# Quarter sums, feature stores and one weight sum of a SwiGLU block are issued at other places

## The chip, the cores and the metric

One NeuronCore of a Trainium2 chip runs the whole block. The metric is the device time of the program in microseconds (us), from its start to its end; lower is better. The engines are named as the profile names them: PE (TensorE, matrix products), PEld (its weight loads), DVE (VectorE), ACT (ScalarE), POOL (GpSimd) and SP (SyncE, which only issues DMAs here). ACTq, SPq and POOLq are the queues of an engine's instructions before they run; a DMA that an engine issues stands in its queue among its other instructions.

## What is computed

One layer of a streaming encoder over 1024 tokens of width 1024, in float32: a normed input projection, eight heads of causal attention with forget gates beside a pooling mixer, an output projection with residual, then a SwiGLU feed-forward with residual and a last norm. The change lies in the feed-forward, of which this is the reference:

```python
def rmsnorm(x, g):
    xf = x.astype(jnp.float32)
    y = xf * lax.rsqrt(jnp.mean(xf * xf, axis=-1, keepdims=True) + EPS)
    return (y * g.astype(jnp.float32)).astype(x.dtype)
...
        h2 = rmsnorm(x, norm2_g[layer])
        gate = jnp.einsum('bsd,df->bsf', h2, w_gate[layer])
        up = jnp.einsum('bsd,df->bsf', h2, w_up[layer])
        x = x + jnp.einsum('bsf,fd->bsd', jax.nn.silu(gate) * up, w_down[layer])
    return rmsnorm(x, final_g)
```

The inner width D_FF is 2816, that is 22 blocks of 128, or 11 pairs of blocks.

## The kernel before

**Precision.** Every float32 product is made of three products of a reduced type. `split` (L119 to L121) writes a high part on ACT (a copy into that type) and a low part on another engine, DVE as a rule (source minus high part). `mm3` (L157 on) then adds high by high (L161), high by low (L162) and low by high (L163) in one PSUM bank. In the profile nearly all matmuls carry these three lines, and all high and low parts L120 and L121. A "page" is the high and the low part of one weight operand.

**Seven products for eight.** Gate and up weights and the normed tokens are cut in two by two blocks, and each such product is made of seven block products instead of eight, P1, P2, P6, P7, P5, P3 and P4. The token operands are made once ("b11", "b21", "t2", "t3", "t1", "b22", "t4"). The weight operands are made anew for each of the 11 pairs `j`: the raw weights `r0` and `r1` come by DMA (`gu_raw`, L1048), POOL forms four sums (`gu_sums`, L1078 on; L1082 to L1085 in the profile), and `gu_page` splits each of the seven operands into one of three pairs of page buffers that take turns. P1 and P2 use raw weights from `r0`, P4 raw weights from `r1`, the others the sums.

**Quarter sums.** From pair 1 on the product P3, the one with the token block b22, is itself made of seven smaller products Q1 to Q7 on quarters (`fine_page`, `fine_product`). For that, b22 is cut once into quarters and their sums: `fine_steps("b22")` (L1182) returns twelve steps, in this order: the wholes of two quarters (L1200: high plus low), their difference (L1207), the split for Q5, a third whole, a difference, the split for Q7, a difference, the split for Q6, a fourth whole, a difference, and the split for Q4, which is written over a quarter of b22 itself. The wholes take slots of the tag "h" of the pool `work`, which has eight slots and also holds the features and some snapshots; Q6 takes "e0" and "e1", which are free by then.

**One step of a pair** (the loop over `todo`, from L1365) makes, in program order: the page of the product two steps ahead (`next_page`), the DMA stores of features that are ready (`spill`, issued on ACT, L1266), the product, and then what follows it (`after`): snapshots of PSUM banks on ACT (L1147), or a corner of the result. A corner (`corner`, L1155 on) has a first add q on DVE (L1166), a SiLU on ACT (L1167), a second add h on DVE (L1168) and their product on POOL (L1169). The corners are h11, h22, h12 and h21; POOL adds them up to the features f1 to f4 (L1173). In pair 0 the corner h22 comes after P7, in later pairs after P5. At the end of a step up to three steps of the list `finer` are run; the list is filled at the end of step P1 of pair 1.

**The down product** is cut the same way, over four groups of pairs, (0, 1), (2, 3, 4), (5, 6, 7) and (8, 9, 10), with the order P1, P2, P6, P7, P5, P4, P3, 28 steps `i` in all; step (b, k) is product k of group b. Each step's page (`down_page`) has a high and a low part of the weight operand and of the feature operand (named d in the profile); it is made one step ahead. Four of the weight operands are differences of raw weights (`down_sum`, L1324): P5's from two raw ones, P6's from P5's, P7's from two raw ones, P4's from P6's. After each of its four row blocks a step adds a PSUM bank onto the residual (L1549 on DVE; the name `added` holds the last).

**Order.** Each engine runs its instructions in the order of its queue. That order is laid out when the program is built, by a planner that keeps the program order as a priority and fills gaps by a simulated timeline. `tc.issue_after(x)` adds one rule: instructions in its block that run on the same engine as x stand behind x in that queue. It adds no wait on another engine. The dictionary `mark` keeps instructions for that use: `mark["hi"]` the last high part in program order, `mark["page"]` the last low part of a page.

Of the kernel before, what the change touches and what calls it, by code (L numbers as in the profile page):

```python
# [11 lines left out]
ALU = mybir.AluOpType  # L12
# [33 lines left out]
def tile_kernel(  # L46
# [16 lines left out]
    nc = tc.nc  # L63
# [24 lines left out]
    def bank(name, tag, bufs, n=1):  # L88
# [11 lines left out]
        out=wmask[:, S - P :],  # L100
# [16 lines left out]
    mark = {}  # L117

    def split(hi, lo, src, eng=nc.vector):  # L119
        mark["hi"] = nc.scalar.activation(out=hi, in_=src, func=AF.Copy)  # L120
        return eng.tensor_tensor(out=lo, in0=src, in1=f32(hi), op=ALU.subtract)  # L121
# [949 lines left out]
    def wk_tile(tag, bufs, name):  # L1071
        return wk.tile([P, 512], F32, tag=tag, bufs=bufs, name=name)
# [85 lines left out]
    def corner(j, name, key, src, to):  # L1158

        h = feature(j, name, to)  # L1160
        q = wk_tile("q" if key else "e2", 1, f"q{name}_{j}")
        if key is None:
            nc.scalar.activation(out=q, in_=banks[src, 0], func=AF.Silu)
            nc.vector.tensor_tensor(out=h, in0=banks[src, 1], in1=q, op=ALU.mult)
        else:
            nc.vector.tensor_tensor(out=q, in0=banks[src, 0], in1=snaps[j, key, 0], op=ALU.add)  # L1166
            nc.scalar.activation(out=q, in_=q, func=AF.Silu)  # L1167
            nc.vector.tensor_tensor(out=h, in0=banks[src, 1], in1=snaps[j, key, 1], op=ALU.add)  # L1168
            nc.gpsimd.tensor_tensor(out=h, in0=h, in1=q, op=ALU.mult)  # L1169

    def feature_sum(j, name, key, a, b, op):
# [9 lines left out]
    def fine_steps(key):  # L1181

        bh, bl = blocks[key]
        spots = dict(Q1=(0, 0), Q2=(1, 0), Q3=(1, 1), Q4=(0, 1))
        for q, (c, h) in spots.items():
            fine[key, q] = quarter(bh, c, h), quarter(bl, c, h)
        t1 = const.tile([P, 2, 2, 256], R, tag="wmask", bufs=1, name=f"fine1_{key}")
        fine[key, "Q5"] = t1[:, 0, :, :], t1[:, 1, :, :]

        def small(pl, tag, name):  # L1190
            return pl.tile([P, 2, 256], R, tag=tag, bufs=1, name=f"{name}_{key}")

        fine[key, "Q6"] = small(wk, "e0", "fine2h"), small(wk, "e1", "fine2l")
        fine[key, "Q7"] = small(wk, "e2", "fine3h"), small(xw, "junk2", "fine3l")
        z = {}

        def whole(c, h):
            def do():
                z[c, h] = wk_tile("h", 8, f"fine_{key}{c}{h}").rearrange("p (c t) -> p c t", c=2)
                nc.vector.tensor_tensor(  # L1200
                    out=z[c, h], in0=f32(quarter(bh, c, h)), in1=f32(quarter(bl, c, h)), op=ALU.add
                )

            return do

        def sub(out, in0, in1):
            return lambda: nc.vector.tensor_tensor(out=z[out], in0=z[in0], in1=z[in1], op=ALU.subtract)  # L1207

        def parts(q, at):
            return lambda: split(*fine[key, q], z[at])  # L1210

        z11, z12, z21, z22 = (0, 0), (0, 1), (1, 0), (1, 1)
        return [
            whole(*z11), whole(*z12), sub(z11, z12, z11), parts("Q5", z11), whole(*z22), sub(z12, z22, z12),
            parts("Q7", z12), sub(z22, z22, z11), parts("Q6", z22), whole(*z21), sub(z21, z21, z22),
            parts("Q4", z21),
        ]

# [121 lines left out]
    def down_page(i):  # L1340
        b, k = steps2[i]
        n = len(GROUPS[b])
        fh, fl, wh, wl = (blk_tile(t, [P, n, 512], R, f"d{i}_{m}") for m, t in enumerate(PAGES[i % 2]))
        split(wh, wl, moving[b, k])
        split(fh, fl, raw2.pop(i))
        stationary[i] = fh, fl, wh, wl

    LATER = ("P1", "P2", "P6", "P7", "P5", "P3a", "P4", "P3b")
    todo = [(j, k) for j in range(NG) for k in (LATER if j else FIRST)]
# [16 lines left out]
    for i, (j, k) in enumerate(todo):  # L1366
        if i + 2 < len(todo):
            next_page(*todo[i + 2])
        if i:
            spill()  # L1370
        if i == 1:
            product(j, k, 0, (0, 1))
            with tc.issue_after(mark["turn", ORDER[-1]].ins):
                product(j, k, 0, (2, 3))
                product(j, k, 1)
        elif i and (k in ("P3a", "P3b") or k == "P4" and j):
            acc = [snaps[j, "sU4", n] for n in range(2)]
            pieces = dict(
                P3a=("Q1", "Q2", "Q7", (0, (0, 1)), (0, (2, 3)), "Q6", "Q4"), P4=((1, (0, 1)), "Q5", (1, (2, 3))),
                P3b=("Q3",),  # L1380
            )
            for piece in pieces[k]:
                with tc.issue_after(mark["mm"].ins):
                    if isinstance(piece, str):
                        fine_product(j, "P3", piece, acc)
                    else:
                        product(j, "P4", *piece)
        elif i:
            for n in range(2):
                product(j, k, n)  # L1390
        if (j, k) == (NG - 1, "P3b"):
            last_features = lambda j=j, k=k: after(j, k)
        else:
            after(j, k)
        if j == NG - 1:
            if k == "P1":
                for par in range(2):
                    down_raw(0, par)
            if k == "P6":
                for key in ("P5", "P6"):  # L1400
                    down_sum(0, key)
            if k == "P7":
                for par in range(2):
                    down_load(par)
            if k == "P3a":
                with tc.issue_after(mark["add"].ins):
                    down_page(0)
        if j == 1 and k == "P1":
            finer += fine_steps("b22")
        for _ in range(min(3, len(finer))):  # L1410
            finer.pop(0)()
        pages.pop((j, k))


# [94 lines left out]
    for i, (b, k) in enumerate(steps2):  # L1509
        g = GROUPS[b]  # L1510
        last_group = b == len(GROUPS) - 1
        more = b + 1 < len(GROUPS)
        if b and k in ("P1", "P2", "P6"):
            with tc.issue_after(added.ins):
                down_sum(b, dict(P1="P6", P2="P7", P6="P4")[k])
        if 0 < i < len(steps2) - 1:
            down_page(i + 1)
        if i + 2 < len(steps2):
            down_load(i + 2)
        if k == "P6" and more:  # L1520
            down_raw(b + 1, 0)
        if k == "P4" and more:
            down_sum(b + 1, "P5")
            down_raw(b + 1, 1)
        fh, fl, wh, wl = stationary.pop(i)
        for c in range(NT // 2):
            ts = slice(c * P, (c + 1) * P)
            kind = 1 if k in ("P1", "P6", "P5", "P3") else 3
            if k in ("P1", "P2", "P7"):
                held[kind, c] = bank(f"d{i}_{c}", *((BANK1[c], 1) if kind == 1 else BANK3[c]))  # L1530
            ps = held[kind, c]
            if last_group and k == "P3" and c == LAST_ROW:
                added, parts, total = last_block(ps, g, ts, (fh, fl, wh, wl))
                final(finished[-1], lambda: nc.vector.scalar_tensor_tensor(
                    out=parts[1], in0=parts[1], scalar=total, in1=parts[0], op0=ALU.add, op1=ALU.add
                ))
                rstds[c] = stat.tile([P, 1], F32, tag="rstd", bufs=4, name=f"rstd_c{c}")
                nc.gpsimd.tensor_tensor(out=rstds[c], in0=parts[1], in1=neg_half, op=ALU.pow)
                finished.append(c)
                continue  # L1540
            for m in range(len(g)):
                with tc.issue_after(closing.ins) if i == 0 else ExitStack():
                    mm3(
                        ps, fh[:, m, ts], fl[:, m, ts], wh[:, m, :], wl[:, m, :],
                        k in ("P1", "P2", "P7") and m == 0, k in ("P2", "P4", "P3") and m == len(g) - 1, True,
                    )
            down, right = ADDS[k]
            row = x2[c + down * NT // 2][:, halves[right]]
            added = nc.vector.tensor_tensor(out=row, in0=ps, in1=row, op=ALU.add)  # L1549
            if last_group and k in ("P6", "P5"):  # L1550
                final_early(c + right * NT // 2)
            if last_group and k in ("P4", "P3"):
                tt = c + down * NT // 2
                final_rms(tt)
                if finished:
                    final(finished[-1])
                finished.append(tt)
# [36 lines left out]
```

## Time and profile before

The median of three runs is 1034.55 us; the profiled execution is another one.

| | us |
|---|---|
| runs: median, lowest, highest | 1034.55, 1034.21, 1035.98 |
| profiled execution | 1034.08 |
| its span, first to last instruction | 1032.3 |
| granted TensorE clock, share of full speed | 0.998 |
| DVE busy | 713.8 |
| ACT busy | 465.4 |
| POOL busy | 405.3 |

Rows of the timeline read: start in us from the span's start, duration, engine, line, operation, tiles written and read, shapes, count; in brackets how long the engine sat idle just before and what ended that. Rows with x2 or more are several instructions merged, from the first start to the last end. The table of waits has, for each pair of waiter and releaser, the total, the number and the longest wait. Matmuls are pipelined: the next starts before the one before it has ended, so what counts on PE is the distance from start to start.

### The profile page before, as it was taken

To read this page: it belongs to the slowest core of one execution; us is meant where nothing else is said; L and a number is where in the kernel's file an instruction comes from. 1 tells how busy PE (TensorE), PEld (TensorE's weight loads), DVE (VectorE), ACT (ScalarE), POOL (GpSimd) and SP (SyncE) were. 2 spreads that over 40 slices of the span, in tenths; PEclk is the share of its full clock that TensorE was granted. 3 is DMA by queue.
4 is the path that set the end of the run, shared out by engine and by line. 5 is a ranking of instruction groups with operands and counts; after the bars stand their busy time and mean duration, and the time that the engine had idled before them with its cause. 6 is when DMAs were issued, how large, how long until landed. Compare 5 with 4: busy or idle time off the path is not lost.

```text
span 1032.3 us, 14700 instructions
## 1 busy us (share of the span) xinstructions
PE 1021.6 (99%) x5284; PEld 873.4 (85%) x5284; DVE 713.8 (69%) x1132; ACT 465.4 (45%) x747; POOL 405.3 (39%) x315
## 2 busy tenths in 40 slices
PE   8999999999999999999999999999999999999997
PEld 7988888998888888888888888888888887888886
DVE  7565566776886479786555455556547899788886
ACT  7434355665665257533343333433334343333346
POOL 4350121214346043356558548557558410000045
PEclk9999999999999999999999999999999999999999
DMA  7224434333742133333243143233326675352424
GB/s 251 53 47 144 105 81 105 82 102 89 242 168 95 49 135 110 93 112 102 102 143 103 63 142 109 76 123 112 92 103 254 215 255 179 123 187 93 153 92 164
DMA packets 108249, 130.25 MB, mean 126 GB/s; under 512 B 7368, under 2 KB 70352, under 8 KB 108176
## 3 DMA queue, kind: packets, MB, share of 16 engines
q1 hardware_dynamic: 96544, 108.18, 33.1%
q10 hardware_dynamic: 11072, 19.69, 5.0%
q0 software_dynamic: 560, 1.44, 0.4%
q8 instruction: 42, 0.69, 0.3%
q14 instruction: 31, 0.25, 0.1%
HBM read 86.29 MB, written 33.03 MB: 116 GB/s over the span
## 4 chain that ended last, share of the span: by engine, by line
PE 48%; DMA 2%; DVE 2%; issue 1%; POOL 1%; ACT 0%; SPq 0%; POOLq 0%; ACTq 0%; DVEq 0%
PE gu_P L163 9%; PE gu_P L162 9%; PE gu_P L161 9%; PE d L162 5%; PE d L161 5%; PE d L163 5%; DMA r_wd<-in_w_down_dram 1%; DVE d L121 1%; DVE x2f_s L1549 1%; DMA r_f<-hsdP 1%; DMA r<-in_w_up_dram 0%; POOL f L1173 0%; DMA hsdP<-f 0%; DVE gu_P_l L121 0%; POOL rstd_c L1462 0%
## 5 line engine op out<-in xcount | busy, mean ns | idle before, releaser
L162 PE MATMUL d<-d,d 128*128 128x512 f32 (+1 forms) x308 | 118.7, 389 | 0.5 <-DVE d L121 0.5
L163 PE MATMUL d<-d,d 128*128 128x512 f32 (+1 forms) x308 | 118.5, 388 | 0.0
L629 POOL TENSOR_SCALAR p<-p,rr 128x128 f32<-128x128 f32 (+3 forms) x64 | 48.8, 767 | 175.8 <-DVE rr L628 141.9
L161 PE MATMUL d<-d,d 128*128 128x512 f32 x308 | 107.8, 388 | 0.0
L120 ACT ACTIVATE d<-r_f 128x1536 fp32r<-128x1536 f32 (+1 forms) x28 | 38.8, 1384 | 109.4 <-PE d L162 109.3
L1169 POOL TENSOR_TENSOR h<-h,qh 128x512 f32<-128x512 f32 x33 | 63.6, 1927 | 34.7 <-ACT qh L1167 26.8
L1082 POOL TENSOR_TENSOR s<-r 128x1024 f32<-128x1024 f32 x10 | 24.0, 2403 | 133.0 <-DVE gu_P3b_l L121 46.3
L121 DVE TENSOR_TENSOR gu_P_l<-r,gu_P_h 128x1024 fp32r<-128x1024 f32 x32 | 54.7, 1711 | 30.0 <-ACT gu_P_h L120 30.0
L120 ACT ACTIVATE gu_P_h<-r 128x1024 fp32r<-128x1024 f32 x32 | 33.9, 1061 | 85.3 <-issue 43.4
L1450 POOL TENSOR_SCALAR sse<-sse 128x1 f32<-128x1 f32 x7 | 3.5, 494 | 167.1 <-ACT junk L1446 167.1
L162 PEld LDWEIGHTS d<-d,d 128*128 128x128 f32 x308 | 57.8, 188 | 13.1 <-DVE d L121 1.1
L161 PEld LDWEIGHTS d<-d,d 128*128 128x128 f32 x308 | 57.8, 188 | 12.0
L163 PEld LDWEIGHTS d<-d,d 128*128 128x128 f32 x308 | 57.8, 188 | 11.8
L121 DVE TENSOR_TENSOR gu_P_l<-s,gu_P_h 128x1024 fp32r<-128x1024 f32 (+1 forms) x38 | 51.7, 1369 | 18.9 <-ACT gu_P_h L120 18.8
L626 ACT ACTIVATE p<-p,mn 128x128 f32<-128x128 f32 (+3 forms) x64 | 49.4, 773 | 31.9 <-DVE mn L620 30.2
L648 DVE TENSOR_TENSOR tl<-tp,th 128x512 fp32r<-128x512 f32 (+1 forms) x80 | 49.5, 633 | 9.4 <-ACT th L647 8.2
L121 DVE TENSOR_TENSOR d<-r_f,d 128x1536 fp32r<-128x1536 f32 (+1 forms) x28 | 47.7, 1703 | 6.2 <-ACT d L120 6.2
L163 PE MATMUL qk<-hTh,l_qk 128*128 128x512 f32 x128 | 50.7, 396 | 0.0
L161 PE MATMUL qk<-hTh,h_qk 128*128 128x512 f32 x128 | 50.6, 395 | 0.0
L162 PE MATMUL qk<-hTl,h_qk 128*128 128x512 f32 x128 | 50.4, 394 | 0.0
L1167 ACT ACTIVATE qh<-qh 128x512 f32<-128x512 f32 x33 | 20.9, 633 | 64.3 <-POOL f L1173 32.6
L647 ACT ACTIVATE th<-tp 128x512 fp32r<-128x512 f32 (+1 forms) x80 | 42.6, 550 | 16.0 <-PE tp L643 13.1
(802 smaller groups left out, 3235.8 us busy)
## 6 DMA issues: line engine op xcount, KB each, us to landing
r_f<-hsdP SPq DMA_DIRECT2D x77, 256.0 KB
r_wd<-in_w_down_dram SPq DMA_DIRECT2D x22, 512.0 KB
r<-in_w_gate_dram SPq DMA_DIRECT2D x21, 512.0 KB
r<-in_w_up_dram SPq DMA_DIRECT2D x21, 512.0 KB
hsdP<-f ACTq DMA_DIRECT2D x40, 256.0 KB
s<-hi SPq DMA_DIRECT2D x64, 128.0 KB
hsdP<-h ACTq DMA_DIRECT2D x32, 256.0 KB
x<-in_x_dram SPq DMA_DIRECT2D x8, 512.0 KB
```

The source lines that it names most:

```text
L120: mark["hi"] = nc.scalar.activation(out=hi, in_=src, func=AF.Copy)
L121: return eng.tensor_tensor(out=lo, in0=src, in1=f32(hi), op=ALU.subtract)
L161: nc.tensor.matmul(ps, lh, rh, start=start, stop=False, **kw)
L162: nc.tensor.matmul(ps, lh, rl, start=False, stop=False, **kw)
L163: mark["mm"] = nc.tensor.matmul(ps, ll, rh, start=False, stop=stop, **kw)
L626: nc.scalar.activation(out=pr[:, :n], in_=pr[:, :n], func=AF.Exp, scale=-1.0, bias=mn, accum_out=rs)
L629: nc.gpsimd.tensor_scalar(out=pr[:, :n], in0=pr[:, :n], scalar1=rr, scalar2=1.0, op0=ALU.mult, op1=ALU.mult)
L647: nc.scalar.activation(out=th[:, :w], in_=tp[:, :w], func=AF.Copy)
L648: nc.vector.tensor_tensor(out=tl[:, :w], in0=tp[:, :w], in1=f32(th[:, :w]), op=ALU.subtract)
L1082: g(out=s1, in0=a21, in1=a22, op=ALU.add)
L1167: nc.scalar.activation(out=q, in_=q, func=AF.Silu)
L1169: nc.gpsimd.tensor_tensor(out=h, in0=h, in1=q, op=ALU.mult)
```

## The change

There are four edits, all of them about the place of instructions in the queues; the arithmetic stays.

1. The list of twelve quarter steps is filled at the end of step P4 of pair 0 instead of P1 of pair 1. Two steps are run there, behind the second add of pair 0's h22 on DVE. In pair 1 three are run at the end of P1 and of P2 and two at the end of P6 and of P7, each group behind the low part of the page that was made in the same step: P6, P7, P5 and P3a.
2. The first two wholes take the tags "e0" and "e1" instead of two slots of "h"; Q6's tiles, on the same tags, are asked for only when its step is run.
3. `spill` stands behind the last high part in program order on ACT.
4. The down sum for P5 of group 1 moves from step (0, P4) to step (1, P1), where it and the sum for P6 stand behind both low parts of the page made in that step (that of (1, P2)). For groups 2 and 3 nothing changes.

```diff
-            nc.vector.tensor_tensor(out=h, in0=banks[src, 1], in1=snaps[j, key, 1], op=ALU.add)
+            mark[name, j] = nc.vector.tensor_tensor(out=h, in0=banks[src, 1], in1=snaps[j, key, 1], op=ALU.add)
...
-        fine[key, "Q6"] = small(wk, "e0", "fine2h"), small(wk, "e1", "fine2l")
...
-                z[c, h] = wk_tile("h", 8, f"fine_{key}{c}{h}").rearrange("p (c t) -> p c t", c=2)
+                at = ("h", 8) if c else (f"e{h}", 1)
+                z[c, h] = wk_tile(*at, f"fine_{key}{c}{h}").rearrange("p (c t) -> p c t", c=2)
...
         def parts(q, at):
-            return lambda: split(*fine[key, q], z[at])
+            def do():
+                if q == "Q6":
+                    fine[key, q] = small(wk, "e0", "fine2h"), small(wk, "e1", "fine2l")
+                split(*fine[key, q], z[at])
+
+            return do
...
-        split(wh, wl, moving[b, k])
-        split(fh, fl, raw2.pop(i))
+        low = split(wh, wl, moving[b, k])
+        lows = low, split(fh, fl, raw2.pop(i))
         stationary[i] = fh, fl, wh, wl
+        return lows
...
         if i:
-            spill()
+            with tc.issue_after(mark["hi"].ins):
+                spill()
...
-        if j == 1 and k == "P1":
+        if (j, k) == (0, "P4"):
             finer += fine_steps("b22")
-        for _ in range(min(3, len(finer))):
-            finer.pop(0)()
+        for _ in range(min(3 if j and k in ("P1", "P2") else 2, len(finer))):
+            with tc.issue_after((mark["page"] if j else mark["h22", 0]).ins):
+                finer.pop(0)()
...
-        if b and k in ("P1", "P2", "P6"):
+        if b and k in ("P1", "P2", "P6") and (b, k) != (1, "P1"):
             with tc.issue_after(added.ins):
                 down_sum(b, dict(P1="P6", P2="P7", P6="P4")[k])
         if 0 < i < len(steps2) - 1:
-            down_page(i + 1)
+            lows = down_page(i + 1)
+        if (b, k) == (1, "P1"):
+            with tc.issue_after(lows[0].ins), tc.issue_after(lows[1].ins):
+                for key in ("P5", "P6"):
+                    down_sum(b, key)
...
         if k == "P4" and more:
-            down_sum(b + 1, "P5")
+            if b:
+                down_sum(b + 1, "P5")
             down_raw(b + 1, 1)
```

## The prediction, made before the changed kernel ran

> **What bounds the kernel now.** I read the head of the page first, then the table of TensorE's waits, then the timeline where a wait falls into the part that the change touches. The page says whose kernel this is:
>
> ```profile
> span 1032.3 us, 14700 instructions
> PE 1021.6 (99%) x5284; PEld 873.4 (85%) x5284; DVE 713.8 (69%) x1132; ACT 465.4 (45%) x747; POOL 405.3 (39%) x315
> ```
>
> TensorE (PE) is busy in all but 10.7 us of the span. So no edit to another engine can pay unless it ends a wait of PE, and no edit can cost unless it makes one. The view of waits lists all that PE has:
>
> ```profile
> PE warm L254 <- DVE junk L252: 1.2, 1, 1.2
> PE tr_a L150 <- DVE x L300: 0.8, 1, 0.8
> PE d L162 <- DVE d L121: 0.5, 1, 0.5
> PE gu_P L163 <- DVE gu_P_l L121: 0.5, 1, 0.5
> PE v L374 <- ACT hTh L152: 0.4, 1, 0.4
> PE spread L264 <- DVE gcol L260: 0.3, 1, 0.3
> ```
>
> Four of the six belong to the opening lines, which the diff leaves alone. Two lie where it works: a page of the gate/up products (gu_P) and a page of the down products (d), each waiting for a low part on VectorE (DVE). Their real price is read from the starts of the matmuls:
>
> ```profile
> 479.49 0.39 PE L162 MATMUL gu_P<-b21l,gu_P_h 128*128 128x512 f32 x1
> 480.33 0.50 PE L163 MATMUL gu_P<-b21h,gu_P_l 128*128 128x512 f32 x1 [0.45 <-DVE gu_P_l L121]
> 480.67 0.40 PE L161 MATMUL gu_P<-b21h,gu_P_h 128*128 128x512 f32 x1
> ...
> 852.85 0.39 PE L161 MATMUL d<-d,d 128*128 128x512 f32 x1
> 853.74 0.50 PE L162 MATMUL d<-d,d 128*128 128x512 f32 x1 [0.50 <-DVE d L121]
> 854.07 0.40 PE L163 MATMUL d<-d,d 128*128 128x512 f32 x1
> ...
> 870.12 0.91 PE d L161 x4
> ```
>
> The last row (from the chain of waits) gives the pace: four matmuls in 0.91 us, 0.23 us from start to start. At 479.49 the next start was due at 479.72 and came at 480.33: 0.61 us lost; the one after it came after 0.34 instead of 0.23: 0.11 more. At 852.85 the next was due at 853.08 and came at 853.74: 0.66, then 0.10. **First stall 0.72 us, second 0.76 us, together 1.48 us**, or 0.14% of the time. That is the whole stake on the good side.
>
> **What makes the first stall.** Going back from it, engine by engine:
>
> ```profile
> 463.23 1.22 DVE L121 TENSOR_TENSOR gu_P_l<-r,gu_P_h 128x1024 fp32r<-128x1024 f32 x1
> 464.89 0.58 SPq L1048 DMA_DIRECT2D r<-in_w_up_dram  x1
> 469.82 2.41 POOL L1082 TENSOR_TENSOR s<-r 128x1024 f32<-128x1024 f32 x1 [15.28 <-DMA r<-in_w_up_dram]
> 472.18 3.39 POOL L1084 TENSOR_TENSOR s<-r,r 128x1024 f32<-128x1024 f32 x1
> 475.53 1.29 POOL L1169 TENSOR_TENSOR h<-h,qh 128x512 f32<-128x512 f32 x1
> 476.85 0.33 ACTq L1266 DMA_DIRECT2D hsdP<-h  x1
> 477.28 1.06 ACT L120 ACTIVATE gu_P_h<-r 128x1024 fp32r<-128x1024 f32 x1 [6.51 <-POOL h L1169]
> 478.37 1.90 DVE L121 TENSOR_TENSOR gu_P_l<-r,gu_P_h 128x1024 fp32r<-128x1024 f32 x1 [4.73 <-ACT gu_P_h L120]
> ...
> 499.64 1.22 DVE L121 TENSOR_TENSOR gu_P_l<-r,gu_P_h 128x1024 fp32r<-128x1024 f32 x1
> 514.68 1.89 DVE L121 TENSOR_TENSOR gu_P_l<-r,gu_P_h 128x1024 fp32r<-128x1024 f32 x1 [2.37 <-ACT gu_P_h L120]
> ```
>
> The low part of pair 1's page P4 (463.23) frees the weight buffer, the load of pair 2 follows, POOL forms two sums and only then h22, the store of h22 stands on ACT's queue ahead of the high part of pair 2's page P2, and the low part of that page (478.37 to 480.27) is what PE awaited. The last two rows are the same two low parts one pair later, where PE doesn't wait: 15.04 us apart, against 15.14 here. So the chain has a fixed length, and what is late is its start. The low part must end at 479.72 less its 0.06 us of handover (480.27 to 480.33): **page P4's low part must come 0.61 us earlier**.
>
> What stands ahead of it on DVE are the quarter sums of b22, the "fine" tiles:
>
> ```profile
> 450.31 1.89 DVE L1200 TENSOR_TENSOR fine_b<-b22h,b22l 128x512 f32<-128x512 f32 x2
> 452.71 2.38 DVE L1200 TENSOR_TENSOR fine_b<-b22h,b22l 128x512 f32<-128x512 f32 x2
> 455.62 1.21 DVE L121 TENSOR_TENSOR gu_P_l<-s,gu_P_h 128x1024 fp32r<-128x1024 f32 x1
> L1207 DVE TENSOR_TENSOR fine_b<-fine_b,fine_b x4: 680/682/682, 455.0 to 459.2; 128x512 f32<-128x512 f32 x4
> ```
>
> Twelve instructions: four adds (4.27 us), four subtractions (0.68 each) and four low parts of the same size; they and the pages fill DVE from 450.31 to 463.23.
>
> **The change, part by part.** The order on each engine is laid out at build time and the trace cannot show the new one, so each part gets bounds.
>
> *Two adds begin in pair 0, behind h22's second add.* They leave the crowded stretch (1.89 us) and go into a place where DVE sits idle (next fence: 2.58 us before 430.63). Their tiles move from the shared "h" slots to e0 and e1, which nothing else uses by then, so they wait for no store. Queued behind them on DVE are h22's first add, h12 and pair 1's first low parts; ACT waits for these and PE for the low parts. Cost at PE: nothing, with the idle time as cover; if that cover fails, see the slower rival.
>
> *The other ten go three, three, two, two, each group behind a page.* After page P5's low part (455.62) seven of the twelve ran before page P4's; now only the last four are asked for there (one for Q6, a whole, a difference, one for Q4). Three fewer by 0.68 is 2.0 us. Lower bound of what page P4 gains: nothing, if its high part on ACT sets the time; upper bound: those 2.0 and the 1.89, 3.9 us. I take 2.0, which has a row for each instruction; 0.61 is needed. Value: 0.72 us, all or nearly nothing. PE first uses the results in pair 1's step P3a, and none is moved behind a page later than that step's own.
>
> *Stores behind high parts.* The edge asks that a store follow the high part of the page made in the same step. For h22 of pair 1 that is the page P3b:
>
> ```profile
> 465.62 0.83 ACT L120 ACTIVATE gu_P3b_h<-s 128x768 fp32r<-128x768 f32 x1
> ```
>
> Its store is at 476.85, already behind. The same holds for the stores of every step that I followed in pairs 0 to 2. So the edge binds nothing in the order that the trace shows: value 0, and the 6.51 us that ACT waits at 477.28 stay. Were the stores to move after all, a store could issue one high part (about 1 us) later, or a high part earlier by up to those 6.51 us; neither reaches PE while the low part is in time. What would queue behind a late store is the reuse of the "h" slots by snapshots and features.
>
> *One down sum later.* P5's sum of group 1 moves from the end of group 0 to behind both low parts of page 8, with P6's, two sums then in a row:
>
> ```profile
> 839.81 1.75 DVE L1324 TENSOR_TENSOR sumP<-r_wd 128x1536 f32<-128x1536 f32 x1
> ...
> 847.38 1.49 ACT L120 ACTIVATE d<-r_f 128x1536 fp32r<-128x1536 f32 x1 [3.52 <-PE d L162]
> 848.78 1.47 ACT L120 ACTIVATE d<-r_wd 128x1536 fp32r<-128x1536 f32 x1
> 849.67 1.75 DVE L121 TENSOR_TENSOR d<-r_f,d 128x1536 fp32r<-128x1536 f32 x1
> 851.93 1.75 DVE L121 TENSOR_TENSOR d<-r_wd,d 128x1536 fp32r<-128x1536 f32 x1
> ...
> 866.73 1.75 DVE L121 TENSOR_TENSOR d<-sumP,d 128x1536 fp32r<-128x1536 f32 x1
> ```
>
> DVE has no gap from the first of these to the second stall. Without 1.75 us ahead, page 7's last low part would end at 853.68 - 1.75 = 851.9, if DVE alone sets it. What is late next is ACT: the first high part ends at 848.87, so the pair of low parts (2.26 us from start to start, then 1.75) ends at 852.9 at the latest. PE is due at 853.08, so the stall goes in both cases: 0.76 us, with 0.2 us to spare in the worse.
>
> The price comes one page later. Queued behind the two sums are the adds of step (1,P1), P7's sum and page 9; PE waits for page 9. Its last low part ends at 868.48 and PE needs it at 870.12 + 0.91 = 871.03: 2.55 us to spare. One more sum takes 1.75 and PE, no longer stalled, comes 0.76 sooner: 0.04 us remain if DVE gains nothing earlier, 0.8 if it starts as much earlier as PE does. Cost 0, upper bound some tenths. SP's queue and POOL's get no DMA more or less: the loads of the raw tiles still wait for P7's sum, as before.
>
> **Sum.** -0.72 - 0 - 0.76 = -1.48 us. The profiled execution took 1034.08 us (1.8 more than its span): 1032.60. The median of the runs is 1034.55, 0.47 above that execution; 1034.55 - 1.48 = **1033.1 us**.
>
> **A rule that speaks against it.** DVE and POOL hold each other up:
>
> ```profile
> 430.63 0.69 DVE L1166 TENSOR_TENSOR qh<-gu_P,sn_sU 128x512 f32<-128x512 f32 x1 [2.58 <-POOL h L1169]
> 432.18 2.41 POOL L1083 TENSOR_TENSOR s<-s,r 128x1024 f32<-128x1024 f32 x1 [1.58 <-DMA r<-in_w_up_dram]
> 433.20 5.81 DVE L121 TENSOR_TENSOR gu_P_l<-r,gu_P_h 128x1024 fp32r<-128x1024 f32 x2 [1.28 <-ACT gu_P_h L120]
> 437.59 0.39 PE L163 MATMUL gu_P<-b11h,gu_P_l 128*128 128x512 f32 x1
> ```
>
> Two low parts of pair 1 took 5.81 us beside POOL's sums; one of that size took 1.21 at 455.62. [...]
>
> **The rivals.**
>
> *B, one stall stays* (the rest of the fine work still stands before page P4's low part, or the order in the down stage eats its 0.2 us): 1034.55 - 0.74 = 1033.8. For it: the first gain rests on an order that I can't see. Against it: three times the needed time is freed.
>
> *C, nothing changes* (page P4 hangs on ACT, and page 9 takes over the stall): 1034.5. For it: the 0.04 us, and the stores that are behind already. Against it: both would have to fail at once.
>
> *D, slower: the two early adds land beside POOL.* Place: DVE's queue between h12 and pair 1's first low part. The first of the two low parts at 433.20 ends about half way, 436.1; PE needs it at 437.59, so 1.5 us are to spare. Each add may wait for one POOL sum and run: 2.41 + 0.68 = 3.1 us. One such add costs 1.6 at PE, 1034.7 in all; both cost 4.7, 1034.55 - 1.48 + 4.7 = 1037.8. It decides from 3.0 us of delay on: below, the gains cover it. For it: the 5.81 us row. Against it: the 2.58 us idle before 430.63, nearer to the instruction that they follow.
>
> **How the numbers follow.** Forecast 58%, B 21%, C 12%, D with both adds 7%, unseen 2%. About 0.2% (2.07 us) is what a measurement of this kernel can tell from no change; the whole stake is 1.48, so even the full gain stays inside, and only a run-to-run shift of 0.6 us puts it outside: 12% for faster. Slower needs D or the unseen: 8%. The rest, 80%, is the same. The range takes the forecast with 0.8 us of spread below it, B and C, and 0.8 above C: 1032.3 to 1035.3; D is left out.
>
> **What would show it.** Right: PE's table of waits keeps the four opening rows only; pair 1's page P4 low part starts by 462.6; two L1200 adds lie near 428; no L1324 before page 7's low parts, two in a row after page 8's; PE's busy time as it is, its span 1.5 us shorter. Wrong: a new wait of PE at page P1 of pair 1 (D), at page P2 of pair 2 (B), at (1,P6) of the down stage (C), or any change in the later pairs, whose order I take as kept.

## The result and the profile after

The changed kernel takes 1032.41 us, median of 14 runs (1032.16 to 1033.88), beside 1034.49 for the kernel before (14 runs, 1033.97 to 1035.98). The ratio is 0.9982, with a 95% interval of 0.9974 to 0.9990: 2.1 us faster by the medians, 1.0 to 2.7 by the interval. The profiled execution took 1032.35 us.

The head of the page after, and under it the whole table of PE's waits (waiter, releaser: total us, number, longest):

```profile
span 1030.5 us, 14701 instructions
PE 1021.7 (99%) x5284; PEld 874.5 (85%) x5284; DVE 716.0 (69%) x1132; ACT 464.9 (45%) x747; POOL 405.2 (39%) x315
...
PE warm L254 <- DVE junk L252: 1.2, 1, 1.2
PE spread L264 <- DVE gcol L260: 0.3, 1, 0.3
PE v L374 <- ACT hTh L152: 0.2, 1, 0.2
```

PE does the same 1021.7 us of work in a span 1.8 us shorter, and both waits of the prediction are gone. The opening's row of `tr_a` is missing too, though no edit touches it; it comes and goes among the profiles (0.8 before, 0.2 to 0.9 in some of the runs below). To see where the time came from, I subtracted the start of each of the 5284 matmuls before from that of its counterpart after (negative: the changed kernel is ahead by that much more):

| where | change of the lead |
|---|---|
| opening, to 8.4 us (not touched; differs from run to run) | -0.13 |
| pair 1, turn of Q4, 468.8 | -0.24 |
| pair 2, page P2, 480.3: the first stall | -0.71 |
| down, page P3 of group 0, 842.8 to 844 | -0.05 |
| down, page (1, P1), 853.7: the second stall | -0.76 |
| last matmul | -1.89 |

The row of 0.24 was not in the prediction. This is the timeline of before there:

```profile
468.29 0.41 DVE L1261 TENSOR_TENSOR sn_sU<-fineB_1P,sn_sU 128x256 f32<-128x256 f32 x1
...
468.53 0.28 PE L163 MATMUL fineA_1P<-fine2h_b,gu_P3b_l 128*128 128x256 f32 x1
468.76 0.39 PE L161 MATMUL fineB_1P<-b22h,gu_P3a_h 128*128 128x256 f32 x1
468.98 0.28 PE L162 MATMUL fineB_1P<-b22l,gu_P3a_h 128*128 128x256 f32 x1
```

Matmuls of this size start 0.12 apart; here two distances are 0.23 and 0.22. The bank fineB was being read by a DVE add until 468.70, late behind the quarter sums. The changed kernel has both distances at 0.12. It is too short for the table of waits, which is why I missed it; the starts show it.

The chain of the first stall after the change, with the two adds and page P4's low part (462.12) at its head; 457.26 is the low part of Q7:

```profile
427.86 3.73 DVE L1200 TENSOR_TENSOR fine_b<-b22h,b22l 128x512 f32<-128x512 f32 x2
431.51 0.68 DVE L1166 TENSOR_TENSOR qh<-gu_P,sn_sU 128x512 f32<-128x512 f32 x1
...
450.69 0.69 DVE L1166 TENSOR_TENSOR qh<-gu_P,sn_sP 128x512 f32<-128x512 f32 x1 [1.18 <-POOL h L1169]
454.42 2.31 DVE L121 TENSOR_TENSOR gu_P_l<-s,gu_P_h 128x1024 fp32r<-128x1024 f32 x1
...
457.26 0.68 DVE L121 TENSOR_TENSOR fine3l_b<-fine_b,fine3h_b 128x512 fp32r<-128x512 f32 x1
...
462.12 1.22 DVE L121 TENSOR_TENSOR gu_P_l<-r,gu_P_h 128x1024 fp32r<-128x1024 f32 x1
...
477.30 1.90 DVE L121 TENSOR_TENSOR gu_P_l<-r,gu_P_h 128x1024 fp32r<-128x1024 f32 x1 [4.72 <-ACT gu_P_h L120]
479.35 0.41 PE L163 MATMUL gu_P<-b21h,gu_P_l 128*128 128x512 f32 x1
```

Page P4's low part starts at 462.12 instead of 463.23, the chain behind it has its length of 15.18 us, and the last low part ends at 479.20, 0.15 before PE starts on it. In the down stage, where page 7 is that of step (1, P1) and page 9 that of (1, P6):

```profile
847.77 1.76 DVE L121 TENSOR_TENSOR d<-r_f,d 128x1536 fp32r<-128x1536 f32 x1 [0.60 <-ACT d L120]
850.04 1.75 DVE L121 TENSOR_TENSOR d<-r_wd,d 128x1536 fp32r<-128x1536 f32 x1
851.94 0.40 PE L162 MATMUL d<-d,d 128*128 128x512 f32 x1
...
866.51 1.74 DVE L121 TENSOR_TENSOR d<-sumP,d 128x1536 fp32r<-128x1536 f32 x1
868.97 0.39 PE L162 MATMUL d<-d,d 128*128 128x512 f32 x1
```

DVE now waits for ACT ahead of page 7 and is done 0.15 us before PE; page 9's low part ends at 868.25, 0.72 us before PE. In the later pairs every engine keeps the order of before.

One question stays after these rows: the traces give 1.73 us (1034.08 - 1032.35), the medians 2.08. So the runs of the kernel before that weren't profiled seem to lose more than the profiled one.

### The profile page after: what moved, and what is told of

Same layout as the page of the kernel before. It is cut to its first block, busy times and chain, and to the rows that moved or that the text cites. A ratio compares the mean times of both kernels' runs of the same rounds, so it can differ in the third digit from the quotient of the medians.

```text
span 1030.5 us, 14701 instructions
## 1 busy us (share of the span) xinstructions
PE 1021.7 (99%) x5284; PEld 874.5 (85%) x5284; DVE 716.0 (69%) x1132; ACT 464.9 (45%) x747; POOL 405.2 (39%) x315
## 4 chain that ended last, share of the span: by engine, by line
PE 98%; DMA 1%; POOL 0%; DVE 0%; issue 0%; ACT 0%; POOLq 0%; ACTq 0%
PE gu_P L162 12%; PE gu_P L161 12%; PE gu_P L163 12%; PE d L161 6%; PE d L162 6%; PE d L163 6%; PE po L657 4%; PE tp L643 3%; PE o L161 3%; PE qk L161 3%; PE qk L163 3%; PE qk L162 3%; PE o L162 3%; PE o L163 3%; PE v L374 2%; PE z L618 2%
## 5 line engine op out<-in xcount | busy, mean ns | idle before, releaser
L1562 DVE TENSOR_TENSOR x2f_s<-d,x2f_s 128x512 f32<-128x512 f32 x64 | 42.3, 682 | 10.0 <-PE d L163 9.9
```

## The experiments

The kernels ran in three groups, each on a chip of its own beside the kernel before, whose medians were 1034.85, 1034.90 and 1034.82; so the groups agree to about 0.1 us (in the measurement of the result it was 1034.49). Each ratio has an interval of about 0.9 us to either side, so the medians alone don't tell some tenths apart; where the time went is read from the traces. The first group is the down sum, the quarter sums, the store edge on the kernel before, and both adds behind h12; the second has the changed kernel's own order (without the store edge, 1032.67) and the three kernels on P5's sum; the rest are the third. What a profile loses at a place is read from the starts of the matmuls.

**The down sum alone** (the kernel before with edit 4).

> The kernel before with the down sums' new steps alone (P5's and P6's sums two steps later). Theory: PE's second stall, 0.76 us at page (1,P1) of down, goes; the first (0.72 at pair 2's page P2) and the small one beside it (0.2 at Q4's turn) stay. Median 1034.49 - 0.76 = 1033.7, span of the profile about 1031.5, and page 9's step keeps some 0.7 us of its 2.55 in hand. Rival 1, the second stall is worth nothing by itself since something behind it waits as long: 1034.5. Rival 2, the whole gain comes from here: 1032.4.

Measured: 1033.42, ratio 0.9987 (0.9978 to 0.9996), 1.43 us under the kernel before. The stall in down is gone from the table of waits, the first is there (0.4). The gain is about twice the 0.76 that the trace had for this edit.

**The quarter sums alone** (edits 1 and 2).

```diff
-                for key in ("P5", "P6"):
-                    down_sum(b, key)
...
-            if b:
-                down_sum(b + 1, "P5")
+            down_sum(b + 1, "P5")
```

> The changed kernel with down's sums in their old steps and the feature stores without their new edge: the quarter sums' new places alone. Theory: the first stall (0.72) and the small loss at Q4's turn (0.24) go, the one in down (0.76) stays: median 1034.49 - 0.96 = 1033.5, and 1033.2 if unprofiled runs lose more there than the profiled one did (what is left of the measured 2.08 when 0.76 is taken off is 1.32). Rival, P4's low part comes earlier but the chain to the h product does not: 1034.5, with the wait of ACT's high part P2 as long as before.

Measured: 1034.47, ratio 0.9994 (0.9985 to 1.0003). A miss: 0.4 us instead of 1.0 to 1.3. The runs spread from 1032.96 to 1035.63, wider than those of the changed kernel. The profile shows where the gain went. At the two places in pairs 1 and 2 PE gains 0.94 us, as expected, and then 0.68 are lost again at 842.6: 0.75 by the starts, where before lost 0.07. The timeline of this kernel, and its table of SP's waits:

```profile
831.84 1.29 SPq L1321 DMA_DIRECT2D r_wd<-in_w_down_dram  x3
839.61 1.76 DVE L1329 TENSOR_TENSOR sumP<-r_wd 128x1536 f32<-128x1536 f32 x1 [0.57 <-DMA r_wd<-in_w_down_dram]
842.56 0.50 PE L162 MATMUL d<-d,d 128*128 128x512 f32 x1 [0.48 <-DVE d L121]
853.55 0.50 PE L162 MATMUL d<-d,d 128*128 128x512 f32 x1 [0.50 <-DVE d L121]
...
SPq L1321 <- DMA hsdP<-f: 1.2, 1, 1.2
```

and the same of the kernel before:

```profile
831.89 1.29 SPq L1316 DMA_DIRECT2D r_wd<-in_w_down_dram  x3
...
SPq L1316 <- DMA hsdP<-f: 0.3, 1, 0.3
...
830.00:834.00 4.00, 4.00 (x19) 3.21 (x19) 4.00 (x6) 2.01 (x2) 0.00 (x0) 1.00 1.01 349
```

(In the last row, of the view by windows, the DMA share and GB/s stand at the end.) P5's sum reads raw rows that SP may only ask for when a feature store has landed. The loads go out at 831.84 and 831.89: the same moment, though PE, DVE and ACT had come there almost a microsecond earlier. SP just waits longer, 1.2 instead of 0.3. The DMA engines are full or nearly so from there on (before 1.01 over these 4 us; here 0.90, then 1.01), and the rows are there at about 839.6. Before, DVE came to the sum at 839.81 and found them there; with PE ahead it comes at 839.04 and waits. So **most of what the first edit gains, the sum in its old place gives back**. Before's own order can meet this too. The kernel of the store edge below has the order of before in this stage, its loads go out at 831.93, and in its profile DVE waits for the rows and PE loses 0.43 us at this place:

```profile
840.09 1.76 DVE L1324 TENSOR_TENSOR sumP<-r_wd 128x1536 f32<-128x1536 f32 x1 [0.29 <-DMA r_wd<-in_w_down_dram]
```

That is a new theory, and its parts were taken one by one on the changed kernel: P5's sum back in its old step; at that place the wait without the work; and the work without the wait.

```diff
-            if b:
-                down_sum(b + 1, "P5")
+            down_sum(b + 1, "P5")
...
+            else:
+                pre = blk_tile(SUMS["P5"], [P, len(GROUPS[1]), 512], F32, "pre")
+                nc.vector.tensor_tensor(
+                    out=pre[:, :, 0:8], in0=moving[1, "b12"][:, :, 0:8],
+                    in1=moving[1, "P1"][:, :, 0:8], op=ALU.subtract)
...
+                with tc.issue_after(prev[1].ins):
+                    nc.vector.tensor_tensor(
+                        out=pre, in0=wd_raw[0][:, :, 0:768], in1=wd_raw[0][:, :, 256:D], op=ALU.subtract)
```

> The changed kernel with P5's sum of group 1 back in its old step, P6's still late. New theory (from the run with the quarter sums alone): the raw rows that P5's sum reads land at about 839.5 whatever PE has gained before, because their loads are issued when the last feature store has landed (831.8 in both) and all DMA engines are busy by then; so DVE waits for them at the old place, and PE pays once at about 842.5 (0.6 us) and again at 853.5 (0.76). Time 1032.4 + 1.4 = 1033.8, up to 1034.5 where the rows land later. Rival, the moved sum is worth 0.76 wherever PE stands: 1033.2, with no stall at 842.

> The changed kernel with, at the place where P5's sum was, a subtraction of 8 columns of each row block of the same two operands (written into P5's tile, which the real sum overwrites later): the wait for the raw rows without the work. If the wait for the landing is what PE pays: as long as the run with P5's sum in its old step, stalls at 842.5 and 853.5. If wait and 1.75 us of work are needed together: DVE goes on at about 839.6, the low part behind it ends at 840.9 before PE wants it at about 841.8, the delay of 0.8 us is taken up by DVE's 0.6 us of idle time before page 7 but for 0.1 to 0.2: 1032.4 to 1032.6.

> The changed kernel with, at the same place of DVE's queue, a subtraction as large as P5's sum but of raw rows of group 0 that landed long before (its result is overwritten): the work of 1.75 us without the wait. If the work is what PE pays in down: no stall at 842 (low part at 841.7, PE wants it at 841.8), but page 7's low parts come 1.75 - 0.6 = 1.1 us later against 0.15 to spare, a stall of about 0.95 at 852: 1033.3. If only the wait counts: 1032.4.

| on the changed kernel | median | ratio to before (95%) | over the changed order (1032.67) |
|---|---|---|---|
| P5's sum in its old step | 1034.02 | 0.9992 (0.9983 to 1.0001) | 1.35 |
| the wait alone | 1032.63 | 0.9978 (0.9968 to 0.9988) | 0.0 |
| the work alone | 1033.78 | 0.9985 (0.9976 to 0.9994) | 1.1 |

All three came out within 0.5 us of what was expected. The timelines of the three in this order:

```profile
839.56 1.76 DVE L1329 TENSOR_TENSOR sumP<-r_wd 128x1536 f32<-128x1536 f32 x1 [0.71 <-DMA r_wd<-in_w_down_dram]
842.51 0.50 PE L162 MATMUL d<-d,d 128*128 128x512 f32 x1 [0.62 <-DVE d L121]
```

```profile
839.11 0.18 DVE L1539 TENSOR_TENSOR pre<-r_wd 128x24 f32<-128x24 f32 x1 [0.25 <-DVE d L121]
847.77 1.76 DVE L121 TENSOR_TENSOR d<-r_f,d 128x1536 fp32r<-128x1536 f32 x1 [0.28 <-ACT d L120]
```

```profile
852.39 1.74 DVE L121 TENSOR_TENSOR d<-r_wd,d 128x1536 fp32r<-128x1536 f32 x1
854.18 0.50 PE L162 MATMUL d<-d,d 128*128 128x512 f32 x1 [0.51 <-DVE d L121]
```

The work alone costs one stall, the one of the prediction (0.78 in this trace). Wait and work together cost that one and another at 842.5 (0.9 and 0.7). The wait alone costs nothing by its median. Its profile is a weak test of that: there the rows had landed by 839.1, with loads issued at 831.86, so DVE stood idle for 0.25 us only, and the idle time ahead of page 7 took up the delay (0.28 left of 0.60). What a wait of 0.6 to 0.7 us would cost without the work, no profile shows. So the second stall is the work's, and the one at 842.5 comes when the work stands behind a late landing; that the wait is harmless without the work rests on the median of eight runs.

**The store edge** was tried twice: put into the kernel before, and taken out of the changed one. Neither alters the order of any engine from the feed-forward on.

```diff
-            spill()
+            with tc.issue_after(mark["hi"].ins):
+                spill()
```

> The kernel before with the feature store's new edge alone (the store behind the high part). Theory: every engine's order of work is the same as before, so 1034.5 and both stalls as before (0.72 and 0.76). Rival, the edge frees ACT's high part P2 from the store that stands ahead of it (1.3 us of the chain): the first stall goes and the time is 1033.8.

> The changed kernel without the feature stores' new edge: the order of work on all five engines is that of the changed kernel. Expected 1032.4, PE's waits those of the opening alone, the first stall and the one in down gone; it is also the changed kernel's time beside the other three runs on this chip. Rival, the edge has a part in the gain: PE stalls again at pair 2's page P2 and the time is up to 0.7 longer.

Measured: 1034.36 with it on the kernel before (ratio 0.9997, 0.9988 to 1.0006), and 1032.67 without it on the changed one (0.9977, 0.9968 to 0.9986). No effect shows, as forecast. The trace of the second, though, is 1.5 us late from 270 us on, long before anything that was changed. Its timeline, and that of the changed kernel at the same place:

```profile
269.26 1.06 ACT L120 ACTIVATE h_wo<-r_wo 128x1024 fp32r<-128x1024 f32 x1 [2.38 <-DMA r_wo<-in_w_out_dram]
270.37 0.73 PE L161 MATMUL o<-h_wo,h_mix 128*128 128x512 f32 x2 [0.77 <-ACT h_wo L120]
```

```profile
267.56 1.06 ACT L120 ACTIVATE h_wo<-r_wo 128x1024 fp32r<-128x1024 f32 x1 [0.69 <-DMA r_wo<-in_w_out_dram]
269.42 0.63 PE L161 MATMUL o<-h_wo,h_mix 128*128 128x512 f32 x2
```

A load of output weights landed 1.7 us later in that execution. The same place is late in the profiles of six of these kernels, by 0.5 to 1.5 us. Three of the ten runs of this kernel are 0.7 us or more above its median, and such runs exist of the changed kernel too (1033.28 to 1033.88). It is noise under every number here, and one reason why a single profiled run can't be set against a median.

**Where the early adds may stand.** Rival D of the prediction had them one operation later on DVE, behind h12. First both there, then one:

```diff
-            with tc.issue_after((mark["page"] if j else mark["h22", 0]).ins):
+            with tc.issue_after((mark["page"] if j else mark["h12", 0]).ins):
```

> The changed kernel with the two early adds one operation later on DVE, behind h12's: the place at which the recorded rival D has them. Rival D as recorded: both adds run beside POOL and reach PE with 4.7 us less 1.5 to spare and more, 1037.1 by its own price of 3.2 to 4.7 on the changed kernel's 1032.4. Theory now, from the changed kernel's rows: the first add starts at about 432, the second waits for POOL's sum to about 434.8, pair 1's first low part ends at about 439 instead of 435.8 and the second at about 442, PE wants the first at 437.5: a stall of about 1.4 us, 1033.8. If add and POOL's work do not exclude each other: low part at 437, no stall, 1032.4.

> The changed kernel with one of the two early adds behind h12's operation, the other where it was. By the recorded rival D, one add there costs 1.6 us at PE: 1034.3. By the rows of the run with both there, the add runs 432.2 to 435.0, the low part ends at 437.2 and PE wants it at 437.5: no stall, 1032.7, and the price of two adds (2.4 us of wait and 1.7 at half rate) comes from the second alone.

Measured: both 1034.45 (0.9997, 0.9988 to 1.0006; runs from 1032.60 to 1036.35), one 1033.62 (0.9992, 0.9983 to 1.0001). Both expectations were off. The timeline with one add there:

```profile
432.52 2.42 POOL L1083 TENSOR_TENSOR s<-s,r 128x1024 f32<-128x1024 f32 x1 [0.79 <-DMA r<-in_w_up_dram]
432.97 2.52 DVE L1200 TENSOR_TENSOR fine_b<-b22h,b22l 128x512 f32<-128x512 f32 x1
434.88 2.87 POOL L1084 TENSOR_TENSOR s<-r,r 128x1024 f32<-128x1024 f32 x1
435.41 5.65 DVE L121 TENSOR_TENSOR gu_P_l<-r,gu_P_h 128x1024 fp32r<-128x1024 f32 x2
437.71 2.26 POOL L1169 TENSOR_TENSOR h<-h,qh 128x512 f32<-128x512 f32 x1
438.88 0.50 PE L163 MATMUL gu_P<-b11h,gu_P_l 128*128 128x512 f32 x1 [0.56 <-DVE gu_P_l L121]
```

Read the ends: POOL's sum ends at 434.94, the add, 0.68 us long elsewhere, at 435.49, right behind it. POOL's next sum ends at 437.75, and the first low part, which had been waiting since 435.41, just before 438.88. In these rows the two engines take turns: the add ends 0.55 us behind POOL's sum, the first low part about 1.1 behind the next. So here the add cost the low part behind it not its own 0.68 us but one more turn of POOL, about 2.3 us (435.41 to 437.75). My expectation took the low part's time from the run with both there (2.28 us), in which it had met a shorter instruction of POOL (1.70).

With both there, PE waits longer, and something comes on top (the timeline, and windows with the granted clock ahead of the DMA share):

```profile
440.01 0.50 PE L163 MATMUL gu_P<-b11h,gu_P_l 128*128 128x512 f32 x1 [2.21 <-DVE gu_P_l L121]
440.35 0.40 PE L161 MATMUL gu_P<-b11h,gu_P_h 128*128 128x512 f32 x1
441.37 0.63 PE L162 MATMUL gu_P<-b11l,gu_P_h 128*128 128x512 f32 x1
441.80 0.63 PE L163 MATMUL gu_P<-b11h,gu_P_l 128*128 128x512 f32 x1
...
440.00:441.40 1.40, 1.39 (x6) 1.10 (x7) 1.40 (x1) 0.00 (x0) 1.40 (x1) 0.92 0.32 121
441.40:444.70 3.30, 3.30 (x10) 2.59 (x9) 3.30 (x2) 0.00 (x0) 3.22 (x3) 0.52 0.05 16
```

The wait moved the start by 2.4 us. Then the granted clock falls to about half: it is 0.52 over the 3.3 us of the second window, and the 0.92 of the first says that the fall came some 0.2 us before that window's end, 1.2 us after the restart (an estimate from these two rows). Matmuls start 0.43 apart instead of 0.23. That costs another 1.6. This profiled run was the slowest of its eleven, and one run shows nothing of it; what differs between them wasn't profiled.

**Are the early adds needed, and the pages?** Without the adds in pair 0 (all twelve steps behind pages), and without the edges to the pages:

```diff
-        if (j, k) == (0, "P4"):
+        if (j, k) == (1, "P1"):
             finer += fine_steps("b22")
-        for _ in range(min(3 if j and k in ("P1", "P2") else 2, len(finer))):
+        for _ in range(min(5 if k == "P1" else 3 if k == "P2" else 2, len(finer))):
...
-            with tc.issue_after((mark["page"] if j else mark["h22", 0]).ins):
+            with ExitStack() if j else tc.issue_after(mark["h22", 0].ins):
```

> The changed kernel with none of the quarter sums ahead of pair 1: all of them behind pages, five behind P1's, then three, two and two. Theory: what brings P4's low part forward is that fewer steps are left ahead of it behind the late pages, not the two adds put into pair 0; the adds take DVE's idle 1.18 us before 450.69 instead, P4's low part starts at 462.1 to 462.5 and nothing is lost: 1032.7, as the changed kernel on this chip. Rival, the early adds are what is needed: P4's low part at 463.2 as before, the stall of 0.72 and the 0.24 at Q4's turn are back: 1033.4 to 1033.7.

> The changed kernel with the edges to the pages taken off the quarter sums of pair 1, so that two later steps (subtractions, with a square of ACT between them) move ahead of pair 1's first low part. Theory: that low part ended 1.7 us before PE wanted it (435.76 against 437.49) and two more operations stretched beside POOL cost 1.4 to 4: a stall of up to 2.3 us at 437.5, and PE at half rate behind a stall of over 2 us as in the run with both adds later: 1033 to 1036. Rival, the edges only fix what the queue would do anyway: 1032.7.

Measured: 1034.17 without the early adds (0.9992, 0.9983 to 1.0001), 1034.16 without the edges (0.9994, 0.9985 to 1.0003); each is 1.5 over the changed order. In the first my theory fell. Its timeline, with page P4's low part at 463.89:

```profile
441.50 4.57 DVE L1200 TENSOR_TENSOR fine_b<-b22h,b22l 128x512 f32<-128x512 f32 x2
...
450.33 2.31 DVE L121 TENSOR_TENSOR gu_P_l<-s,gu_P_h 128x1024 fp32r<-128x1024 f32 x1
...
463.89 1.23 DVE L121 TENSOR_TENSOR gu_P_l<-r,gu_P_h 128x1024 fp32r<-128x1024 f32 x1
...
481.00 0.50 PE L163 MATMUL gu_P<-b21h,gu_P_l 128*128 128x512 f32 x1 [0.30 <-DVE gu_P_l L121]
```

In pair 1 the two adds take 4.57 us, again in turns with POOL (its instructions end at 443.83 and 445.53, the second add at 446.07, 0.54 behind); that is more than the idle 1.18 us ahead of the add q at 450.69, and DVE has no gap left. Page P4's low part starts 1.77 later than in the changed kernel, of which 0.66 stem from the opening and from 270 us; the stall is back (0.6 by the starts), with two of 0.1 and 0.4 at 450 and 458 whose releasers the profile doesn't name. Without the edges two more steps get ahead of pair 1's first low part, and PE waits there (0.8 in the table of waits; 1.1 by the starts, and 0.2 more at 434).

**Page 9**, that of step (1, P6), where the prediction had 0.04 to 0.8 us in hand. P4's sum goes ahead of its low parts:

```diff
+                if (b, k) == (1, "P2"):
+                    extra = down_sum(b, "P4")
...
-            lows = down_page(i + 1)
+            with tc.issue_after(extra.ins) if (b, k) == (1, "P2") else ExitStack():
+                lows = down_page(i + 1)
```

> The changed kernel with P4's sum of group 1 moved ahead of page 9's low parts, 1.75 us more work there. The prediction had 0.04 to 0.8 us in hand at that page; the changed kernel's rows show 0.72 (last low part 868.25, PE 868.97). So a stall of 1.75 - 0.72 = 1.0 us at page (1,P6): 1033.7. Rival, page 9 has more in hand than the rows show, since something else is late there: 1032.7.

Measured: 1034.07 (0.9992, 0.9983 to 1.0001); by the starts 1.1 us are lost at that page, 1.0 expected:

```profile
864.48 1.75 DVE L1329 TENSOR_TENSOR sumP<-r_wd,sumP 128x1536 f32<-128x1536 f32 x1
868.41 1.75 DVE L121 TENSOR_TENSOR d<-sumP,d 128x1536 fp32r<-128x1536 f32 x1
870.22 0.50 PE L162 MATMUL d<-d,d 128*128 128x512 f32 x1 [0.85 <-DVE d L121]
```

Not tried: P5's and P6's sums in the new step but not behind both low parts, and other numbers of steps behind each page. No version here is faster than the changed kernel; its only waits of PE are in the opening.

## Why the prediction was right, point by point

**The bound and the stake.** Right in kind: the two stalls went and nothing took their place. The stake was called "together 1.48 us"; the trace gives 1.47 for these two (0.71 and 0.76), and 0.24 more at Q4's turn, which the table of waits doesn't list. The median moved by 2.08, more than "the whole stake", and 1032.41 is 0.1 above the lower end of the range. That it stayed inside is in part luck: the 0.8 us below the forecast were meant for spread, not for a loss that was overlooked.

**"Page P4's low part must come 0.61 us earlier", "I take 2.0".** It came 1.11 earlier. The chain held; the size came out wrong, and so did the count of steps behind page P5's low part. Before there were seven; the prediction has four, the trace shows five (at 456.66, 457.26, 458.04, 459.79 and 461.52), since Q7's low part, asked for ahead of that page, still runs behind it. Two steps fewer are 1.2 us, as they start 0.60 apart and not 0.68; of these 1.0 arrived. What was cleared ahead of the page brought only 0.1: P5's low part starts 1.20 earlier but meets POOL (a product from 454.05 to 455.65) and takes 2.31 us instead of 1.21. The fixed length of the chain (15.04 to 15.14) held at 15.18. Of the supposed abundance 0.15 us remain, as PE itself comes there 0.37 earlier.

**"Cost at PE: nothing, with the idle time as cover".** Right. The adds end at 431.59, 0.88 us late for the next add q, and pair 1's first low part is as early as before. The experiments add that they are needed there, which I had not said. With all twelve steps in pair 1 the same five stand behind P5's low part, yet P4's comes no earlier than before (463.89 less the 0.66 from elsewhere is 463.23), and the stall is back: in pair 1 the two adds cost 4.57 us, in idle time 3.73, of which PE sees nothing. Other ways to spread the steps over pair 1 weren't tried.

**Stores behind high parts, "value 0".** Right, as far as both runs can tell.

**The down sum.** "0.76 us, with 0.2 us to spare in the worse" was right in the trace (0.76; 0.15 to spare, ACT being late next). But the step that moves P5's sum was costed as 1.75 us of work alone. That the sum also waits for raw rows was not asked: before, they landed while DVE was still busy with a low part, and no idle time shows. This is the term that was too small. Taking the edit alone gave 1.43, putting the sum back cost 1.35. The difference between the traces (1.73) and the medians (2.08) probably has the same cause: the landing differs from run to run, and the profiled run of before had it in time. For it speak the profiles with the sum in its old place (0.57 and 0.71 us of waiting in the rows above, none in before's) and above all the profile of before's own order with the store edge, which waits 0.29 there and loses 0.43. It wasn't measured run by run.

**Page 9.** "0.04 us remain if DVE gains nothing earlier, 0.8 if it starts as much earlier as PE does": 0.72, and 1.75 us more work there lost 1.1. The two sums don't stand in a row, as forecast, but with adds of step (1, P1) between them.

**The sum.** The two terms were simply added. They don't add: the quarter sums alone are worth 0.4 by the medians, and 0.75 with P5's sum out of the way (1033.42 against 1032.67). Rival B, "one stall stays", has 1033.8; that is 0.4 too high where the down sum moves alone (1033.42) and 0.7 too low where it is the quarter sums (1034.47).

**Rival D.** Its place was right, and it didn't come true since the adds stand one operation ahead. The 3.1 us for each add (one POOL sum and its own time, 2.41 + 0.68) was the author's estimate and no run shows it: one add there took 2.52 us, both together 5.61. Its prices were 1.6 for one add and 4.7 for both; measured are 0.8 and 4.1 in the traces, about 0.9 and 1.8 in the medians (the profiled run of both was the slowest).

## What to carry to other kernels

When two stalls in a row are taken away, ask at the second what its inputs are tied to: a load that another transfer releases may not come earlier when the engines do (here 831.84 after 831.89), and a wait that another instruction hides in the trace of before comes into the open (0.57 us here). Adds and low parts on DVE beside a busy POOL took a turn of POOL here, not their own duration (2.52 us for an add of 0.68, 2.31 for a low part of 1.21), so the place of two adds decided between no loss at PE and 4.1 us in one trace. Besides the table of waits, compare the starts of the matmuls: small losses (0.24 us at Q4's turn) and slow restarts (1.6 us behind the pause of 2.4) are only there.

## What the runs showed of the hardware

- A pause of PE cost more than itself here. Each of the waits above (matmuls of 512 columns) is followed by one matmul 0.1 us late, 0.34 instead of 0.23 from start to start. Behind the pause of 2.4 us in the run with both adds behind h12 the granted clock was 0.52 for 3.3 us, and matmuls of 512 columns started 0.43 apart. One profiled run shows this; why the clock fell was not shown. Behind the two stalls of before (waits of 0.45 and 0.50 us) it was 1.00, from 480.3 to 485 and from 853.7 to 859. Behind the wait of 0.85 us in the run with P4's sum ahead, 1.1 us were lost and the profiled execution took 1033.65, 1.30 above that of the changed kernel; so no second loss of 1.6 us came on top.
- Beside POOL, instructions of DVE took longer, and in the rows read here the two engines ended by turns. With one add behind h12 that add, 0.68 us long elsewhere, took 2.52 and ended 0.55 us behind POOL's sum. In before a low part, 1.22 us long elsewhere, took 3.42 (from 435.59) and ended 1.08 behind POOL's sum (434.55 to 437.93). Each distance is within 0.15 us of the instruction's own duration. POOL's took longer too: a product h of before 1.29 us at 429.31, with DVE idle, and 2.28 at 437.88, with a low part on DVE.
- Loads in a stretch of full DMA (share 0.9 to 1.0) were awaited for 7.8 to 8.2 us from the first one's issue to the use (831.84 to 839.61; 831.93 to 840.09), in another profile they were there after 7.3 at the latest (831.86 to 839.11), and one load of output weights landed up to 1.7 us later in some executions than in others of the same order of work.
